# The first block of the merge's second gates is computed as the last filler beside the attention, and the second block stands ahead of the merge, in both layers

## The chip, the cores and the metric

The kernel runs on one core of one Trainium2 chip. The metric is the device time of one execution in microseconds (us). Smaller is better.

## The reference

Two layers of a transformer trunk over 512 latent tokens and 256 context tokens, width 1024, float32. Cut to what matters here, a layer is:

```
h = modulate(rms_norm(x))                              # context tokens: hc, same weights
na_q, na_k, na_v, gq, gk, gv, ga, gb = split(h @ w_in) # ga and gb are 1024 wide each
ya = neighbourhood_attention(na_q, na_k, na_v)         # 8 heads of 64
yb = grouped_query_attention(gq, gk, gv)               # 8 heads of 64
merged = sigmoid(ga) * (ya @ w_pa) + sigmoid(gb) * (yb @ w_pb)
x = x + g1 * (merged @ w_o)
x = x + g2 * swiglu(modulate(rms_norm(x)))
```

The context tokens go through the same steps in layer 0. In layer 1, the last, they only give keys and values. So a product over the tokens covers 768 columns (512 and 256) in layer 0 and 512 in layer 1.

## The kernel before

Activations lie transposed, channels on the partitions and tokens along the free dimension. A float32 product is made of three matmuls for each 128 x 128 weight block: every operand is split into a high half (`hi`, written by ACT) and a low half (`lo`, the rest, written by DVE or POOL), and `steps` (L381) issues high x high, high x low and low x high. A weight is loaded raw (tag `wr`, 4 buffers, 512 KB for a block of 128 output channels), its high half is copied by ACT (`wh`, L366, 3 buffers), and its low half is subtracted by POOL or DVE (`wl`, L368, 3 buffers). In the merge, layer 0 uses POOL and layer 1 uses DVE. Buffers of a tag are handed out in a ring, in the order of the program.

**Attention (`mixing`).** TensorE's order is written out by a planner, `Flow`, while the program is built. The attention of the heads, two per step, is the main line: scores (`sc`), transposes of the softmax (`tp`), products with the values (`y`). Each has to wait for ACT or DVE, and the planner keeps a clock with assumed costs to know when. Beside the main line it keeps a list of fillers, generators that do one projection block each in pieces of three matmuls (`pj`, `pv`): nk, nv and nq are keys, values and queries of the neighbourhood heads, gq queries of the other attention, and gb0 to gb7 the eight blocks of the first branch's gate. A filler's piece goes to TensorE in three cases: when the main line would wait by the planner's clock, when the work done by fillers is behind a pace (`pace`, which spreads the cost of the first and the second group of fillers over the grouped-query and the neighbourhood half of the main line, less a `reserve`), and when a head needs a projection that is not done (`force`). Fillers are taken in the order of `PLAN`'s `fill`. What has been begun and is not finished when the main line ends runs then. A finished gate block is kept in one of the 45 slots of 768 columns that all large tiles share.

**Merge (`merge`).** TensorE's order here comes from the scheduler, which places an instruction when it takes it to be ready. First stands one block of the second gate, ga0 (`GA = 1`, the list `ahead`). The four tiles of yb are read back from DRAM (`yb<-yd`, L1542) and split (L393 on ACT, L394 on DVE). Branch 0 multiplies the eight blocks of w_pb with yb (`pp`) and each result with its gate (`mb`, L1571); all eight gates are ready. Then ya is split (L393, L394), and branch 1 does the same with ga and w_pa. For block 0 the gate is ready, for blocks 1 to 7 a projection of the gate (`pj`) comes before the product. The sum of the branches is split into `mh` and `ml`. Beside this, DVE computes sums for the modulation from transposed weights (`wmodT`, L449), whose raw loads use the same ring `wr`. In layer 0 those are two sums for each weight, in layer 1 one. The row vectors that they multiply (`crow`) are loaded once attention's own pool is free.

The output projection (`po`) and the feed-forward part follow, and then the next layer.

Of the kernel before, what the change touches and what calls it, by code (L numbers as in the profile page):

```python
# [42 lines left out]
for _n in ORDER:  # L43
    for _j in range(COLS[_n][1]):
# [18 lines left out]
BEHIND = 3.0  # L63
SLOTS = 45
ATT_P, ATT_PT = 4, 8
GA = 1

MODS = (((0, 1, 1, 1, 1, 1, 1, 1), (1, 2, 2, 2, 2, 2, 1, 0), (1, 1, 1, 1, 1, 1, 1, 0)),
        ((0, 0, 0, 0, 0, 0, 0, 0), (1, 1, 1, 1, 1, 1, 1, 1), (0, 0, 0, 0, 0, 0, 0, 0)))
# [1 line left out]

PLAN = [
    dict(fill=("nk0 nv0 nq0 gq1 gb0 gq2 gb1 gq3 gb2 gb3 nq1",
               "gb4 nk1 gb5 nq2 nk2 nv1 nq3 nk3 gb6 gb7"),
         early=0.9, reserve=8, hop=0.14, move=3.5, soon=0.5, keep=2,
         busy=12, ctx=0.0, vat=(1, 1), load=2, qt=2, rx=2, slow=(1.1, 1.2, 1), banks="gst", lead=(2, 1, 2), quiet=0.0, spared=0),
    dict(fill=("gq1 gb0 nq0 gq2 nv0 gb1 gq3 gb2 nq1 nk0 gb3",
               "nk1 nk2 nq2 nv1 nk3 gb4 nq3 gb5 gb6 gb7"),
         early=0.8, reserve=2, hop=0.2, move=3, soon=0, keep=2,
         busy=2, ctx=1, vat=(1, 1), load=2.5, qt=2, rx=1, slow=(1, 1, 1), banks="tsg", lead=(2, 2, 1), quiet=28.0, spared=2),  # L80
]
# [13 lines left out]
            g=(0.07, 0.00218, "g"), p=(0.0, 0.19, "g"))  # L95
# [236 lines left out]
class Trunk:  # L332
# [1049 lines left out]
    def mixing(self, l, h, last, at, todo, spare):  # L1382
# [3 lines left out]
        spans = joint[:1] if last else joint  # L1386
        n = spans[-1][1]
        plan = self.plan = PLAN[l]
        block = 3 * D * n // P * COL
        whole = 3 * D * T // P * COL  # L1390
        vals, qs, ya, yb, gates = {}, {}, {}, {}, []
        gqs, keys, bias = at.gqs, at.keys, {}
        self.pbufs = dict(s=1, t=3, g=2)
        yd = [self.dpool.tile([P, T], F32, name=f"yd{l}_{j}") for j in range(4)]
        with ExitStack() as stack:
# [5 lines left out]
            pool = self.att = _Bufs(pool_, dict(rx=plan["rx"], qt=plan["qt"], p=ATT_P, pt=ATT_PT))  # L1401

            self.quiet, self.spared = plan["quiet"], plan["spared"]
            if at.rest:
                todo = self.prologue(l, h, spans, spare, at)
# [5 lines left out]
            def gate():  # L1411
                gates.append(self.slot("gt"))
                return gates[-1]

            gq = [Filler(self.gqa_q(l, j, h, spans, pool, gqs), block, 2) for j in range(1, 4)]
            nk = [Filler(self.na_k(l, j, h, joint, keys), whole, 2) for j in range(4)]
            lead = [Filler(g, 0.0, 0, lead=spare) for g, spare in zip(todo, plan["lead"])]
# [2 lines left out]
            nv = [Filler(self.na_v(l, half, h, vals), 2 * whole, 4) for half in range(2)]  # L1420
            nq = [Filler(self.na_q(l, j, h, spans, qs), block, 4) for j in range(4)]
            gb = [Filler(self.gate(l, "gb", j, h, spans, gate, "g"), block, 1, plan["keep"]) for j in range(KB)]
            named = dict(nk=nk, nv=nv, nq=nq, gb=gb, gq=[None] + gq)
            first, second = [[named[w[:2]][int(w[2])] for w in part.split()] for part in plan["fill"]]

            ctx = 0 if last else 8 * 12 * PASS
# [81 lines left out]
            with tc.manual_schedule(engines={mybir.EngineType.PE}):  # L1508
                flow.run(self.attend(items))
            self.flow = None  # L1510
        return [ya[j] for j in range(4)], yd, gates

    def gate(self, l, what, j, h, spans, make, tag):

# [9 lines left out]

        yield from self.project(w, h, spans, evac, tag)

    def merge(self, l, h, ya, yd, gates, spans, pool, beside):

        nc, d = self.nc, self.d
        n = spans[-1][1]  # L1530
        mb = []
        merged = ([], [])
        yb = []

        ahead = []
        for j in range(GA):
            t = pool.tile([P, T], F32, tag="qt", name=self.name("t"))
            drain(self.gate(l, "ga", j, h, spans, lambda: t, "a"))
            ahead.append(t)
        for t in yd:  # L1540
            yb.append(self.slot("yb"))
            nc.sync.dma_start(yb[-1][:, :n], t[:, :n])  # L1542
        for br, (gname, y) in enumerate((("gb", yb), ("ga", ya))):
            yh = ([], [])
            for t in y:
                hi, lo = self.halves(t[:, :n], n)
                yh[0].append(hi)
                yh[1].append(lo)
            for j in range(KB):
                if br == 0 and j < len(gates):  # L1550
                    t = gates[j]
                elif br == 1 and j < len(ahead):
                    t = ahead[j]
                else:
                    t = pool.tile([P, T], F32, tag="qt", name=self.name("t"))
                    drain(self.gate(l, gname, j, h, spans, lambda: t, "a"))
                w = self.weight(d["wp"][l, 1 - br, j], 512, nc.vector if l else None)
                if beside:
                    for _ in range(MODS[l][br][j]):
                        beside.pop(0)()  # L1560
                if br == 0:
                    mb.append(self.slot("mb"))
                else:
                    hi, lo = self.slot("mh", F32R), self.slot("ml", F32R)
                    merged[0].append(hi)
                    merged[1].append(lo)
                for a, b in spans:
                    pp = self.ps("a", "pp")[:, : b - a]
                    self.gemm(pp, w, yh, a, b, 4)
                    if br == 0:  # L1570
                        nc.vector.scalar_tensor_tensor(mb[j][:, a:b], t[:, a:b], 1.0, pp, op0=ALU.add, op1=ALU.mult)  # L1571
                    else:
                        nc.vector.scalar_tensor_tensor(t[:, a:b], t[:, a:b], 1.0, pp, op0=ALU.add, op1=ALU.mult)
                        nc.vector.tensor_tensor(t[:, a:b], t[:, a:b], mb[j][:, a:b], op=ALU.add)
                        nc.scalar.activation(hi[:, a:b], t[:, a:b], AF.Copy)
                        nc.vector.tensor_tensor(lo[:, a:b], t[:, a:b], hi[:, a:b].bitcast(F32), op=ALU.subtract)
        return merged
# [379 lines left out]
    def run(self):  # L1957
# [3 lines left out]
        with (  # L1961
# [23 lines left out]
            for l in range(DEPTH):  # L1985
# [2 lines left out]
                groups = [(0, 256), (256, 512)] if last else joint  # L1988
                n = spans[-1][1]
                nh = n // 2  # L1990
                ya, yd, gates = self.mixing(l, h, last, at, todo, spare)
                self.pbufs = dict(a=6, n=2)
                with (
                    tc.tile_pool(name=f"psMn{l}", bufs=1, space=PSUM, reuse_waits="tile") as psn,
# [19 lines left out]
                    beside = [one(l, n) for n in range(first, ahead)]  # L2014
                    with tc.tile_pool(name=f"m{l}", bufs=1, reuse_waits="tile") as pool_:
                        pool = _Bufs(pool_, dict(rs=2, qt=5), slots)
                        merged = self.merge(l, h, ya, yd, gates, spans, pool, beside)
                        if not last:
                            self.mod_bias(0, 16, 24)
                            self.gates(0, 0)  # L2020
                        x = []
                        for k in range(KB):
                            x.append(self.slot("x"))
                            nc.sync.dma_start(x[k][:, :n], d["x"][k] if l == 0 else xd[k])
                        right, late = self.out_proj(l, merged, x, nh, pool, beside)
# [79 lines left out]
class Quarters:  # L2105
# [14 lines left out]
    def sum(self, key):  # L2120
        v, at = self.t.nc.vector, self.at
        if key == "S1":
            at["S1"] = self.t.fpool.tile([P, D // 2], F32, tag="ws", name=self.t.name("ws"))[:, : self.n]
            v.tensor_tensor(at["S1"], at["A21"], at["A22"], op=ALU.add)
        elif key == "S2":
            assert "A11" in self.halves
            at["S3"], at["S2"] = at["A21"], at["A11"]
            v.tensor_tensor(at["S3"], at["A11"], at["A21"], op=ALU.subtract)
            v.tensor_tensor(at["S2"], at["S1"], at["A11"], op=ALU.subtract)  # L2129
        elif key == "S4":  # L2130
            assert "A12" in self.halves
            at["S4"] = at["A12"]
            v.tensor_tensor(at["S4"], at["A12"], at["S2"], op=ALU.subtract)
# [170 lines left out]
```

## Time and profile before

| | |
|---|---|
| median of 3 runs | 1966.19 us (1964.42 to 1966.62) |
| profiled execution | 1967.19 us |
| its span, first to last instruction | 1965.1 us |
| mean granted TensorE clock | 0.996 |
| DMA | 214.78 MB, mean 109 GB/s |

PE is TensorE's matmuls, PEld its weight loads, DVE is VectorE, ACT is ScalarE, POOL is GpSimd, and SP is the queue that issues the DMAs. Each profile line of an instruction has its start in us from the span's start, its length, the engine, the line of the kernel, the operation, what it writes and reads, the shape and a count. In brackets stands the idle time before it on its engine, and what ended it. PE's lengths overlap, since matmuls are pipelined. In the trace of before, layer 0's attention ends at about 413 us and its merge at about 551; in layer 1 these are about 1453 and 1542.

### The profile page before, as it was taken

The page shows a single profiled execution, that of the slowest core. Times are in us where ns is not written, and L with a number is a line of the kernel's source. Part 1 is how long each engine was busy: PE and PEld are TensorE (multiplying, and loading weights), DVE is VectorE, ACT ScalarE, POOL GpSimd, SP SyncE. Part 2 cuts the span into 40 slices and gives each one's busy share as a digit, 9 for nine tenths or more (in the row PEclk, how much of TensorE's full clock was granted, in tenths as well). Part 3 has the DMA queues.
Part 4 walks back from the last instruction along what each step waited for, and adds up shares of the span by engine and source line. Part 5 has one row for each costly group of instructions (what it writes and reads, how often), then busy time and mean ns, then how long its engine had stood idle before and what let it go on. Part 6 is the DMA issues. An engine that isn't in the chain of part 4 may idle for free.

```text
span 1965.1 us, 31571 instructions
## 1 busy us (share of the span) xinstructions
PE 1920.8 (98%) x12298; PEld 1777.7 (90%) x12298; DVE 1479.8 (75%) x2813; ACT 948.9 (48%) x1832; POOL 220.1 (11%) x130
## 2 busy tenths in 40 slices
PE   8999999999999999999999999999999999999998
PEld 8989999888899999999999888889888999988997
DVE  7468887788768888786867587879566587876785
ACT  5456666642236534242524255667453364544454
POOL 0332212213200000000000013222300000000000
PEclk9999999999999999999999999999999999999999
DMA  8121112244452143434453422112235532233333
GB/s 324 44 71 41 52 57 63 76 148 166 144 207 86 65 132 127 124 107 138 137 161 116 129 86 60 52 49 78 67 93 196 176 112 77 95 112 96 94 109 108
DMA packets 73109, 214.78 MB, mean 109 GB/s; under 512 B 8704, under 2 KB 10880, under 8 KB 72960
## 3 DMA queue, kind: packets, MB, share of 16 engines
q1 hardware_dynamic: 72960, 212.78, 33.2%
q8 instruction: 96, 1.57, 0.3%
q14 instruction: 53, 0.43, 0.1%
HBM read 200.69 MB, written 6.82 MB: 106 GB/s over the span
## 4 chain that ended last, share of the span: by engine, by line
PE 66%; DVE 6%; issue 3%; ACT 2%; DMA 0%; POOL 0%; DVEq 0%; POOLq 0%; ACTq 0%
PE po L381 19%; PE qu L1726 13%; PE pj L381 10%; PE qv L1726 7%; PE pp L381 4%; PE qc L1726 3%; PE pf L381 3%; PE pv L954 1%; PE sc L1037 1%; PE y L1073 1%; PE tp L1063 1%; PE sc L1164 1%; PE y L1200 1%; DVE w L1593 1%; PE tp L1188 1%
## 5 line engine op out<-in xcount | busy, mean ns | idle before, releaser
L1726 PE MATMUL qu<-r,w 128*128 128x384 f32 (+1 forms) x1872 | 295.4, 310 | 1.9 <-ACT tt L1732 1.9
L1726 PEld LDWEIGHTS qu<-r,w 128*128 128x128 f32 x1872 | 281.1, 189 | 6.5 <-ACT tt L1732 2.7
L381 PE MATMUL pj<-h,wh 128*128 128x512 f32 (+1 forms) x704 | 257.5, 366 | 5.2 <-ACT kg L813 1.7
L366 ACT ACTIVATE wh<-wr 128x1024 fp32r<-128x1024 f32 (+2 forms) x157 | 146.1, 935 | 213.8 <-issue 67.2
L381 PE MATMUL pj<-h,wl 128*128 128x512 f32 (+1 forms) x704 | 247.6, 352 | 0.0
L381 PE MATMUL pj<-hl,wh 128*128 128x512 f32 (+1 forms) x704 | 247.0, 351 | 0.0
L381 PE MATMUL po<-ph,wh 128*128 128x512 f32 (+1 forms) x576 | 197.8, 344 | 2.6 <-ACT wh L366 1.6
L381 PE MATMUL po<-ph,wl 128*128 128x512 f32 (+1 forms) x576 | 196.4, 342 | 2.1 <-DVE wl L368 1.4
L381 PE MATMUL po<-pl,wh 128*128 128x512 f32 (+1 forms) x576 | 195.8, 340 | 0.0
L1589 ACT ACTIVATE w<-wr 128x512 fp32r<-128x512 f32 x234 | 145.4, 625 | 103.5 <-DVE wr L2129 39.3
L368 POOL TENSOR_TENSOR wl<-wr,wh 128x1024 fp32r<-128x1024 f32 (+1 forms) x66 | 144.6, 2194 | 392.8 <-ACT wh L366 392.7
L1581 DVE SCALAR_TENSOR_TENSOR x<-po,G,x 128x256 f32<-128x256 f32 (+3 forms) x168 | 99.1, 596 | 113.4 <-PE po L381 112.4
L1593 DVE TENSOR_TENSOR w<-wr,w 128x512 fp32r<-128x512 f32 x234 | 159.6, 685 | 14.9 <-ACT w L1589 13.6
L1726 PE MATMUL qv<-r,w 128*128 128x384 f32 (+1 forms) x936 | 151.1, 310 | 1.7 <-ACT tt L1732 1.7
L381 PEld LDWEIGHTS pj<-h,wh 128*128 128x128 f32 x704 | 134.0, 190 | 20.2 <-ACT kg L813 1.9
L381 PEld LDWEIGHTS pj<-h,wl 128*128 128x128 f32 x704 | 133.4, 189 | 18.2
L381 PEld LDWEIGHTS pj<-hl,wh 128*128 128x128 f32 x704 | 134.2, 191 | 13.8
L1726 PEld LDWEIGHTS qv<-r,w 128*128 128x128 f32 x936 | 141.1, 190 | 2.8 <-ACT tt L1732 2.7
L1013 ACT ACTIVATE pth<-tp 128x512 fp32r<-128x512 f32 x176 | 103.4, 595 | 65.3 <-PE tp L1063 37.7
L509 POOL TENSOR_TENSOR rs<-rs,expo 128x2 f32<-128x2 f32 (+2 forms) x8 | 6.2, 773 | 1116.7 <-DVE rs L508 1116.7
L1014 DVE TENSOR_TENSOR ptl<-tp,pth 128x512 fp32r<-128x512 f32 x176 | 119.5, 685 | 15.1 <-ACT pth L1013 13.4
L381 PEld LDWEIGHTS po<-ph,wh 128*128 128x128 f32 x576 | 108.4, 188 | 17.5 <-ACT wh L366 3.5
(249 smaller groups left out, 4321.2 us busy)
## 6 DMA issues: line engine op xcount, KB each, us to landing
wr<-wfi SPq DMA_DIRECT2D x88, 512.0 KB, 3.3
wr<-wmodT SPq DMA_DIRECT2D x84, 512.0 KB, 3.3
wr<-win SPq DMA_DIRECT2D x68, 512.0 KB, 3.3
wr<-wfo SPq DMA_DIRECT2D x64, 256.0 KB, 2.7
wr<-wo SPq DMA_DIRECT2D x26, 512.0 KB, 3.6
wr<-wfo SPq DMA_DIRECT2D x26, 384.0 KB, 3.3
wr<-wp SPq DMA_DIRECT2D x32, 256.0 KB, 2.9
x<-x SPq DMA_DIRECT2D x16, 384.0 KB, 6.4
```

The lines of the kernel that those rows point to most:

```text
L366: nc.scalar.activation(hi, raw, AF.Copy)
L368: (eng or nc.gpsimd).tensor_tensor(lo, raw, hi[:].bitcast(F32), op=ALU.subtract)
L381: nc.tensor.matmul(ps[:, : b - a], u[:, c], v[k][:, a:b], start=(k == 0 and i == 0), stop=(k == nk - 1 and i == 2),)
L954: nc.tensor.matmul(ps[:, t * 256 : t * 256 + 256], a[k][:, tok], b[:, c], start=(k == 0 and i == 0), stop=(k == KB - 1 and i == 2))
L1013: nc.scalar.activation(hi, tp, AF.Copy)
L1014: nc.vector.tensor_tensor(lo, tp, hi[:].bitcast(F32), op=ALU.subtract)
L1037: nc.tensor.matmul(s[:, lo:up], qt[:, b * P : (b + 1) * P], kk[k][:, lo:up], start=(k == 0 and (b % 2 == 0 or lo > 0)), stop=(k == 1), ski ...
L1063: nc.tensor.transpose(tp[:, (2 * j + b) * P : (2 * j + b + 1) * P], ps_[b][:, (k + j) * P : (k + j + 1) * P], self.ident)
L1581: self.nc.vector.scalar_tensor_tensor(x[j][:, f:u], ps[:, f - a : u - a], self.G[l][i][:, s, j : j + 1], x[j][:, f:u], op0=ALU.mult, op1=A ...
L1589: self.nc.scalar.activation(t[:, :n], src, AF.Copy)
L1593: self.nc.vector.tensor_tensor(t[:, n : 2 * n], src, t[:, :n].bitcast(F32), op=ALU.subtract)
L1726: nc.tensor.matmul(banks[bank], u[:, c], v, start=(first and k == 0 and i == 0), stop=(k == kn - 1 and i == 2), skip_group_check=True)
```

## The change

One block of ga moves into the list of fillers of both layers, as the last one. It is kept in a slot (list `others`) and handed to `merge` as the first entry of `ahead`. The block that `merge` computes before its loops is now ga1. Branch 1 finds the gates of blocks 0 and 1 ready and computes six. `GA[l]` is the pair of the blocks beside attention and the blocks ahead of the merge.

```diff
-GA = 1
+
+GA = (1, 1), (1, 1)
...
     dict(fill=("nk0 nv0 nq0 gq1 gb0 gq2 gb1 gq3 gb2 gb3 nq1",
-               "gb4 nk1 gb5 nq2 nk2 nv1 nq3 nk3 gb6 gb7"),
+               "gb4 nk1 gb5 nq2 nk2 nv1 nq3 nk3 gb6 gb7 ga0"),
...
     dict(fill=("gq1 gb0 nq0 gq2 nv0 gb1 gq3 gb2 nq1 nk0 gb3",
-               "nk1 nk2 nq2 nv1 nk3 gb4 nq3 gb5 gb6 gb7"),
+               "nk1 nk2 nq2 nv1 nk3 gb4 nq3 gb5 gb6 gb7 ga0"),
...
+            def other():
+                others.append(self.slot("gt"))
+                return others[-1]
...
+            ga = [Filler(self.gate(l, "ga", j, h, spans, other, "g"), block, 1, plan["keep"]) for j in range(GA[l][0])]
+            named = dict(nk=nk, nv=nv, nq=nq, gb=gb, ga=ga, gq=[None] + gq)
...
-    def merge(self, l, h, ya, yd, gates, spans, pool, beside):
+    def merge(self, l, h, ya, yd, gates, ahead, spans, pool, beside):
...
-        ahead = []
-        for j in range(GA):
+        for j in range(GA[l][0], sum(GA[l])):
             t = pool.tile([P, T], F32, tag="qt", name=self.name("t"))
             drain(self.gate(l, "ga", j, h, spans, lambda: t, "a"))
             ahead.append(t)
...
-                        merged = self.merge(l, h, ya, yd, gates, spans, pool, beside)
+                        merged = self.merge(l, h, ya, yd, gates, others, spans, pool, beside)
```

More of the change, by code (lines that the diff above doesn't have):

```diff
@@ L1390, in mixing @@
         whole = 3 * D * T // P * COL
-        vals, qs, ya, yb, gates = {}, {}, {}, {}, []
+        vals, qs, ya, yb, gates, others = {}, {}, {}, {}, [], []
         gqs, keys, bias = at.gqs, at.keys, {}
@@ L1422, in mixing @@
             gb = [Filler(self.gate(l, "gb", j, h, spans, gate, "g"), block, 1, plan["keep"]) for j in range(KB)]
-            named = dict(nk=nk, nv=nv, nq=nq, gb=gb, gq=[None] + gq)
+            ga = [Filler(self.gate(l, "ga", j, h, spans, other, "g"), block, 1, plan["keep"]) for j in range(GA[l][0])]
+            named = dict(nk=nk, nv=nv, nq=nq, gb=gb, ga=ga, gq=[None] + gq)
             first, second = [[named[w[:2]][int(w[2])] for w in part.split()] for part in plan["fill"]]
@@ L1510, in mixing @@
             self.flow = None
-        return [ya[j] for j in range(4)], yd, gates
+        return [ya[j] for j in range(4)], yd, gates, others
     def gate(self, l, what, j, h, spans, make, tag):
@@ L1990, in run @@
                 nh = n // 2
-                ya, yd, gates = self.mixing(l, h, last, at, todo, spare)
+                ya, yd, gates, others = self.mixing(l, h, last, at, todo, spare)
                 self.pbufs = dict(a=6, n=2)
```

## The prediction

> **What bounds the kernel now.** First the page's busy shares, then one table of stretches around the two places where attention ends and the branch merge begins, then the chain of waits, then TensorE's own timeline there. In the table the columns behind the stretch are its length, the busy time of PE, weight loads, DVE, ACT and POOL, the granted PE clock, the DMA share and GB/s.
>
> ```profile
> PE 1920.8 (98%) x12298; PEld 1777.7 (90%) x12298; DVE 1479.8 (75%) x2813; ACT 948.9 (48%) x1832; POOL 220.1 (11%) x130
> ```
> ```profile
> 407.40:413.30 5.90, 4.21 (x28) 3.42 (x27) 5.79 (x10) 4.85 (x10) 1.92 (x1) 0.96 0.23 77
> 413.30:416.60 3.30, 3.30 (x11) 2.63 (x10) 1.01 (x3) 1.28 (x2) 0.00 (x0) 0.56 0.81 259
> 423.00:456.60 33.60, 33.60 (x195) 29.66 (x194) 31.01 (x49) 7.23 (x11) 13.03 (x8) 1.00 0.55 188
> 456.60:464.05 7.45, 6.14 (x27) 4.49 (x25) 7.32 (x13) 2.64 (x4) 1.29 (x1) 1.00 0.38 122
> 1459.20:1481.10 21.90, 21.89 (x97) 17.80 (x95) 13.62 (x20) 7.18 (x11) 0.00 (x0) 1.00 0.42 129
> 1481.10:1482.50 1.40, 0.40 (x2) 0.35 (x3) 1.40 (x4) 1.40 (x4) 0.00 (x0) 1.00 0.86 312
> ```
>
> TensorE is busy 98% of the span, and the change neither adds nor removes a matmul. So only TensorE's idle and slow time can be won or lost, 44.3 us of the span in all, and of that only what lies near the moved work. In layer 0 the tail of attention (407.40 to 413.30) has 1.69 us idle, and the 3.30 us behind it run at a clock of 0.56. The first branch (423.00 to 456.60) is full, and between the branches 1.31 us are idle (456.60 to 464.05) with DVE busy 7.32 of 7.45. Layer 1 has only the small hole of 1.00 us at 1481.
>
> **The change part by part.** *The price of a block.* The chain of waits gives start, length, work:
>
> ```profile
> 471.36 4.18 PE pp L381 x24
> 475.54 8.34 PE pj L381 x48
> ...
> 1453.15 6.18 PE pj L381 x27
> ...
> 1493.28 5.44 PE pj L381 x24
> 1498.71 2.72 PE pp L381 x12
> ```
>
> A gate block (pj) is 8.34 us of TensorE in layer 0 and 5.44 in layer 1; a branch product (pp) is 4.18 and 2.72. Before, ga0 stands between attention and the first branch and ga1 to ga7 in the second branch. After, ga0 is the last filler of attention, ga1 stands between, and six blocks remain behind. Each block brings its 512 KB load, an ACT copy for the high half (below the one of ga1, at 452.42), a low half and a tanh for each span:
>
> ```profile
> 452.42 1.06 ACT L366 ACTIVATE wh<-wr 128x1024 fp32r<-128x1024 f32 x1 [3.55 <-PE pp L381]
> 456.60 0.63 ACT L366 ACTIVATE wh<-wr 128x512 fp32r<-128x512 f32 x1 [1.65 <-POOL wl L368]
> ```
> ```profile
> L1522 ACT ACTIVATE t<-pj x24: 361/578/599, 420.4 to 1540.3; 128x512 f32<-128x512 f32 x16, 128x256 f32<-128x256 f32 x8
> ```
> ```profile
> L368 POOL TENSOR_TENSOR wl<-wr,wh 128x1024 fp32r<-128x1024 f32 (+1 forms) x66 | 144.6, 2194 | 392.8 <-ACT wh L366 392.7
> ...
> wr<-win SPq DMA_DIRECT2D x68, 512.0 KB, 3.3
> ```
>
> Inside attention the low half goes to POOL in both layers (late in layer 1 too), about 2.2 us on an engine that works 11% of the span; in layer 1 that takes one such operation from DVE. I cost these at nothing: they run ahead under the last blocks of gb. Without that cover ga0 would start up to 3.3 + 1.06 + 2.2 = 6.6 us late. The extra slot that ga0 holds (one of 45) is also costed at nothing: the reload of yb could be held back by it, but ga1's 8.34 us still stand ahead of the first branch.
>
> *Where ga0 goes, layer 0.* The fillers run out before attention does:
>
> ```profile
> 407.29 0.28 PE L381 MATMUL pj<-h,wl 128*128 128x256 f32 x1
> 407.42 0.60 PE L1112 MATMUL tp<-ident_sb,p 128*128 128x128 f32 x4
> 407.83 0.77 PE L1200 MATMUL y<-pth,v 128*128 128x256 f32 x5
> ...
> 410.22 0.51 PE L1122 MATMUL y<-pth,v 128*128 128x256 f32 x2 [0.24 <-DVE ptl L1014]
> 410.56 0.40 PE L1122 MATMUL y<-ptl,v 128*128 128x256 f32 x2
> 412.13 0.47 PE L1122 MATMUL y<-pth,v 128*128 128x256 f32 x2 [1.17 <-DVE y L1024]
> 412.76 0.79 PE L1122 MATMUL y<-ptl,v 128*128 128x256 f32 x2 [0.16 <-DVE ptl L1014]
> 413.35 0.63 PE L381 MATMUL pj<-h,wh 128*128 128x512 f32 x1
> ```
>
> The last piece of gb7 is at 407.29. After it stand the last transposes and value products with three waits, and ga0 only from 413.35. The two heads that need nq3 and nk3 force all fillers before gb6 to be done, in both versions, so that point is the same and what follows it is filled by waits: gb6 and gb7 are used up at 407.29 as before, and ga0 then goes into the waits. A piece of it is three matmuls. The idle here is 1.69 us; in layer 1, where fillers do not run out, the same kinds of pieces take 1.10 (ten y) and 0.46 (four tp):
>
> ```profile
> 1448.40 1.10 PE y L1200 x10
> 1449.51 0.46 PE tp L1188 x4
> ```
>
> So the 5.93 us from 407.42 to 413.35 would need 2 x 0.46 + 1.10 + about 0.9 for the eight y of L1122 (estimate, 8/10 of 1.10) = 2.9; the loss is between the 1.69 shown idle and 3.0. I take 2.2 gained, since the longest wait (1.17) comes from DVE being late with the halves of yb, which the filling plan does not count, and may not be asked to cover.
>
> *The slow stretch.* The first matmul of ga0 is 0.63 long; at 0.56 of the clock 3.30 us hold 3.30 x 0.44 = 1.45 us too much. It follows a stretch with 71% busy (4.21 of 5.90). If that is filled the clock should stay: 1.4 gained, bounds 0 and 1.45. The Trainium skill, TensorE: Matmul & The Clock Gate, "HAM oscillation — how this bites in real kernels", puts the limit at idle gaps above about 3.4 us. No single gap here is above 1.17 us and the clock fell all the same, so the trace does not agree; by that rule the slow stretch would not hang on these gaps and would stay, and the sum below would be -0.8 instead of -2.2. I go by the row.
>
> *Between the branches, layer 0.* What is late next is the split of ya on DVE, which the second branch needs:
>
> ```profile
> 457.72 0.50 PE L381 MATMUL pj<-h,wh 128*128 128x512 f32 x1 [0.73 <-DVE mb L1571]
> 464.05 0.50 PE L381 MATMUL pp<-lo,wh 128*128 128x512 f32 x1 [0.58 <-DVE lo L394]
> ```
> ```profile
> 454.96 2.10 DVE L449 CUSTOM_DVE_ANT_0 junk<-wr,crow 128x1024 f32<-128x1024 f32 x1 [2.13 <-DMA wr<-wmodT]
> 463.05 0.95 DVE L394 TENSOR_TENSOR lo<-y,hi 128x768 fp32r<-128x768 f32 x1
> ```
> ```profile
> 447.31 0.33 SPq L357 DMA_DIRECT2D wr<-win  x1
> 447.74 0.37 SPq L357 DMA_DIRECT2D wr<-wp  x1
> 451.61 0.81 SPq L357 DMA_DIRECT2D wr<-wmodT  x2
> ```
>
> Before, TensorE ran out of branch-0 products at 456.60, did the first span of ga1 (from 457.72), and met the first low half of ya at 464.05. After, ga1 has been done earlier and cannot stand here. But the first branch ends later: 456.60, plus 8.34 for ga1, minus 3.6 (2.2 + 1.4) from the tail = 461.3. DVE's queue of modulation sums starts from attention's last transposes, not from ga0's end, so it does not move with them, and its 2.13 us wait for a load goes, because ga1's raw weight (447.31) leaves the four-buffer load ring in front of those two loads: low half at 464.05 - 2.1 = 461.9. On the other side, the ring is emptied by TensorE's progress through branch 0, and could hold the sums back by up to the 8.34 - 3.6 = 4.7 us that TensorE is later, giving 468.8 less 2.1 = 466.7. Idle between the branches is then 0.6 to 5.4 us against 1.31. I take 1.5, near the early end, since DVE is the fuller engine there (31.01 of 33.60) and the extra time goes to it first: +0.2. The time of ga1's first span is not lost: it was spent before.
>
> *Between the branches, layer 1.*
>
> ```profile
> 1482.10 0.50 PE L381 MATMUL pp<-hi,wh 128*128 128x512 f32 x1 [1.01 <-ACT hi L393]
> 1482.44 0.40 PE L381 MATMUL pj<-h,wh 128*128 128x512 f32 x1
> ```
> ```profile
> 1481.44 2.18 ACT L393 ACTIVATE hi<-y 128x512 fp32r<-128x512 f32 x4
> ```
> ```profile
> 1482.96 2.49 DVE L394 TENSOR_TENSOR lo<-y,hi 128x512 fp32r<-128x512 f32 x4
> ```
>
> TensorE waits 1.01 us for the upper half of ya, does one matmul, then ga1 while DVE makes the lower halves. After, no gate is ready in that place: ga2's weights need the ring buffer that the last product of branch 0 frees. The second matmul waits for the first lower half, 1482.96 + 2.49/4 = 1483.6, that is 2.5 us after 1481.10 less the one matmul of 0.3: 2.2 idle instead of 1.0, +1.2. Bounds: -1.0 (halves come in time because the scheduler places them earlier) and +2.7 (1.2 and a clock drop of 1.45 as at 413.30). Layer 1's tail of attention gains nothing: the chain has 27 pj without a hole there, three of gb7 and ga0.
>
> *The rest of attention.* The second group of fillers is longer by one block and is handed out faster. That could fill, or make, waits like these, 1.0 each; I take 0, bounds -2.0 and +2.0:
>
> ```profile
> PE tp L1188 <- DVE z L1007: 1.0, 1, 1.0
> ```
> ```profile
> PE pv L954 <- DVE ql L988: 1.0, 1, 1.0
> ```
>
> *The sum*: -2.2 - 1.4 + 0.2 + 1.2 + 0 = -2.2 us. The profiled run took 1967.19 us (span 1965.1 and 2.1 around it), 1.0 above the median of the runs, 1966.19. Set against the median: 1964.0. Less than 0.2% (3.9 us) is about what a measurement of this kernel cannot tell from no change.
>
> **The rivals.** *Everything closes (0.25).* The halves of ya come in time in both layers and the tail closes fully: -3.0 - 1.45 - 1.31 - 1.01 = -6.8, with attention's own waits down to -8.8: 1957.4 to 1962, middle 1960. For it: DVE has a third of its time free in layer 1's first branch (13.62 of 21.90), and the halves of ya are ready to be made long before. Against it: they were ready early in this version too, and were placed at the branch's end.
>
> *The cover is lost (0.14), on the slower side.* One place: the start of layer 0's second branch. If the splits of ya keep their distance from branch 0's end, TensorE stands 7.45 us where ga1 stood, 6.1 more than now, and the clock drops behind it (+1.4). With layer 1's +1.2 and the tail's -3.6 that is +5.1: 1971.3. It decides once the lower half comes 3.7 us behind the last product of branch 0 (3.6 - 1.2 + 1.3, where the sum is zero); from 6.2 on, with the clock drop, the loss passes 0.2%. For it: the next gate, ga2, can't fill in early, since its copy comes only at the ring's turn at branch 0's end, as at 456.60, and another 2.2 us on POOL follow. Against it: 2.13 us of DVE's delay is a load that comes sooner now.
>
> *Nothing moves (0.13).* The plan sees no wait in layer 0's tail, runs ga0 behind the last value product as the merge did, and the gap between the branches absorbs the rest: -1 to +1.5, 1966.
>
> **How the numbers follow.** The forecast has 0.48, its own range 1962 to 1966.5. Faster by over 0.2% (under 1962.3) is the first rival and 0.06 of the forecast: 0.31. Slower by over 0.2% (over 1970.1) is most of the second: 0.12. Within: 0.57. The range for 8 in 10 runs from 1959.0, inside the first rival, to 1970.0, which leaves most of the second out.
>
> **What would show it.** Right: in layer 0 pieces of pj stand between the last tp and y, no stretch at 0.56 follows, two gates' worth of pj precede the first pp, and TensorE idles 1 to 3 us where the second branch begins, waiting for lo. In layer 1 the wait of pp for hi turns into one for lo, 2 us or so. Wrong: a wait of over 5 us for lo in layer 0, a clock drop behind either gap, ga0 waiting for its weights, yb reloaded so late that the first pp waits, or new waits inside attention's second half.

## The result, and the profile after

The changed kernel takes 1969.84 us (median of 18 runs, 1965.38 to 1974.34), the kernel before 1965.11 us (18 runs, 1961.82 to 1966.62). The ratio is 1.0025, 95% interval 1.0019 to 1.0031: slower by 4.7 us, where 2.2 us faster was forecast. The profiled execution of after took 1967.43 us (span 1965.7), only 0.24 us more than that of before; why the two profiles hide the difference is told below.

Stretches of the two kernels from landmark to landmark (those called before and after are the kernel before and the changed one): end of layer 0's scores to the first branch product, from there to the first product of out_proj, then for layer 1 the last value product to the first branch product, and from there to out_proj. The columns are those of the prediction's table. Before:

```profile
401.70:423.00 21.30, 19.61 (x122) 17.38 (x121) 16.57 (x29) 12.56 (x27) 1.92 (x1) 0.92 0.35 120
423.00:550.50 127.50, 126.19 (x723) 110.67 (x722) 103.85 (x159) 33.48 (x56) 37.92 (x21) 1.00 0.46 157
1452.90:1459.20 6.30, 6.30 (x31) 5.24 (x30) 3.67 (x7) 3.75 (x8) 0.00 (x0) 1.00 0.36 125
1459.20:1542.10 82.90, 81.89 (x362) 67.48 (x361) 51.87 (x74) 29.67 (x44) 0.00 (x0) 1.00 0.48 159
```

After:

```profile
402.20:428.20 26.00, 26.00 (x173) 23.73 (x172) 14.55 (x29) 14.47 (x30) 2.58 (x2) 1.00 0.39 134
428.20:551.00 122.80, 119.12 (x674) 104.47 (x674) 107.71 (x160) 31.96 (x53) 37.10 (x20) 0.99 0.47 159
1449.00:1459.30 10.30, 10.30 (x48) 8.58 (x47) 3.82 (x7) 4.14 (x7) 0.00 (x0) 1.00 0.65 205
1459.30:1542.40 83.10, 78.71 (x337) 64.34 (x337) 50.47 (x73) 28.09 (x41) 0.00 (x0) 0.96 0.47 152
```

A gate block is 8.34 us in layer 0 and 5.44 in layer 1. Six blocks instead of seven remain in each merge, so the two should have come out at 127.5 - 8.34 = 119.2 and 82.9 - 5.44 = 77.5 us. They took 122.8 and 83.1: 3.6 and 5.6 us were lost in them. The loss lies where the branches meet. There, in after:

```profile
407.40:418.30 10.90, 10.90 (x73) 9.85 (x72) 4.25 (x11) 4.95 (x11) 1.29 (x1) 1.00 0.59 208
461.85:480.00 18.15, 14.47 (x66) 11.65 (x65) 17.43 (x30) 3.16 (x4) 3.29 (x2) 0.91 0.48 166
1481.30:1500.00 18.70, 14.35 (x53) 11.39 (x54) 9.71 (x15) 6.47 (x10) 0.00 (x0) 0.82 0.42 139
```

The tail of layer 0's attention (407.40 to 418.30) is now full at full clock, as forecast. But 3.68 of the 18.15 us behind branch 0 of layer 0 are idle, and 4.35 of the 18.70 us behind that of layer 1, and the clock falls to 0.91 and 0.82 there.

**Layer 0's boundary.** TensorE, ACT and DVE in after:

```profile
466.50 0.50 PE L382 MATMUL pj<-h,wh 128*128 128x512 f32 x1 [2.86 <-ACT wh L367]
458.18 1.56 ACT L394 ACTIVATE hi<-y 128x768 fp32r<-128x768 f32 x2
465.39 1.06 ACT L367 ACTIVATE wh<-wr 128x1024 fp32r<-128x1024 f32 x1 [5.65 <-DMA wr<-win]
466.09 0.95 DVE L395 TENSOR_TENSOR lo<-y,hi 128x768 fp32r<-128x768 f32 x1
```

TensorE ends branch 0 at about 462. The first low half of ya has its turn in DVE's queue only at 466.09 and is done at 467.04, 5 us later, although ACT made the high halves from 458.18 on. In the kernel before the low half came even later after branch 0's end (456.60 to 464.00), but ga1's product stood in between. Matmuls of ga2 are written ahead of the product that needs the low half, so TensorE also waits for ga2's weight. In this profile that wait of 2.86 us ended at 466.50 with ACT's copy, for whose load ACT had waited 5.65 us, and the low half came 0.5 us behind it: both were late. The load was itself issued only at 460.93, after the load queue had waited 2.9 us for DVE, whose sum begun at 458.70 ended just before.

**Layer 1's boundary.** TensorE, ACT, DVE and the load queue in after:

```profile
1483.11 0.73 PE L382 MATMUL pp<-hi,wh 128*128 128x512 f32 x2 [1.85 <-ACT hi L394]
1486.85 0.79 PE L382 MATMUL pj<-h,wl 128*128 128x512 f32 x1 [2.54 <-DVE wl L369]
1481.48 1.06 ACT L367 ACTIVATE wh<-wr 128x1024 fp32r<-128x1024 f32 x1 [2.49 <-DMA wr<-win]
1482.44 2.17 ACT L394 ACTIVATE hi<-y 128x512 fp32r<-128x512 f32 x4
1484.42 1.22 DVE L450 CUSTOM_DVE_ANT_0 wr<-wr,crow 128x1024 f32<-128x1024 f32 x1 [2.43 <-DMA wr<-wmodT]
1485.58 1.22 DVE L369 TENSOR_TENSOR wl<-wr,wh 128x1024 fp32r<-128x1024 f32 x1
1486.71 2.49 DVE L395 TENSOR_TENSOR lo<-y,hi 128x512 fp32r<-128x512 f32 x4
1477.27 0.33 SPq L358 DMA_DIRECT2D wr<-win  x1
1479.93 0.33 SPq L358 DMA_DIRECT2D wr<-wmodT  x1
```

Here the queues are in the way. ga2's raw weight is issued at 1477.27. ACT waits 2.49 us for it, with ya's high halves queued behind its copy: TensorE idles 1.85 us. DVE waits 2.43 us for a load of the sums that was issued at 1479.93, behind ga2's weight, and has ga2's low half and then ya's low halves queued behind that: TensorE idles 2.54 us more.

**Why the profiles look equal.** TensorE's clock drops in one execution and not in another, for a few us at a time, behind waits that both have: in layer 1's attention TensorE waits 1.66 us until about 1204 and 1.91 us until about 1295, in both profiles (until 1204.38 and 1295.70 in before, 1203.78 and 1293.50 in after). The stretches around these waits in the profile of before:

```profile
1200.00:1205.00 5.00, 3.34 (x26) 3.09 (x25) 2.62 (x9) 3.73 (x7) 1.64 (x1) 0.97 0.00 0
1205.00:1210.00 5.00, 5.00 (x30) 4.60 (x30) 3.59 (x9) 3.38 (x7) 0.00 (x0) 0.69 0.02 5
1290.00:1295.00 5.00, 3.78 (x31) 3.39 (x29) 4.78 (x9) 2.22 (x5) 0.00 (x0) 1.00 0.24 54
1295.00:1300.00 5.00, 4.30 (x21) 4.01 (x22) 3.61 (x9) 2.50 (x5) 0.00 (x0) 0.69 0.00 0
```

and, behind the same two waits, in that of after:

```profile
1205.00:1210.00 5.00, 5.00 (x43) 4.86 (x43) 4.69 (x10) 4.57 (x10) 0.00 (x0) 1.00 0.01 3
1295.00:1300.00 5.00, 5.00 (x38) 4.69 (x38) 4.42 (x10) 2.82 (x5) 0.77 (x1) 1.00 0.00 0
```

Layer 1's scores and values took 258.6 us in the profile of before. In three other executions with the same layer 1 they took 255.4, 257.0 and 258.3; with the changed layer 1, in the 15 profiled executions, between 255.3 and 258.8. One profile of each kernel can't show a difference of 4 us in the whole; its stages can.

### The profile page after: what moved, and what is told of

The parts are those of the page before. It is cut to its first block, busy times and chain, and to the rows that moved or that the text cites. A ratio compares the mean times of both kernels' runs of the same rounds, so it can differ in the third digit from the quotient of the medians.

```text
span 1965.7 us, 31561 instructions
## 1 busy us (share of the span) xinstructions
PE 1919.4 (98%) x12298; PEld 1777.2 (90%) x12298; DVE 1480.5 (75%) x2812; ACT 950.3 (48%) x1832; POOL 223.8 (11%) x131
## 4 chain that ended last, share of the span: by engine, by line
PE 66%; DVE 6%; issue 2%; ACT 1%; DMA 1%; POOL 0%; DVEq 0%; POOLq 0%; ACTq 0%
PE po L382 20%; PE qu L1731 13%; PE pj L382 11%; PE qv L1731 7%; PE pp L382 3%; PE qc L1731 3%; PE pf L382 3%; PE pv L955 1%; PE y L1074 1%; PE sc L1038 1%; PE tp L1064 1%; PE y L1201 1%; PE sc L1165 1%; PE tp L1189 1%; DVE w L1598 1%
```

## The experiments

All times are medians beside runs of the kernel before on the same chip; a ratio is to those, with its 95% interval. "Boundary" is the place between the branches, "stage" the time from a layer's first branch product to out_proj's first. The runs are called e1 to e18. What each was expected to show stands ahead of its result.

**1. One layer at a time (e1, e2).** Which layer loses? In e1 layer 1 is unchanged, `GA = (1, 1), (0, 1)` and no ga0 in the second layer's list:

> The change in layer 0 alone; layer 1 is as before (ga0 ahead of the merge, seven blocks behind). Theory M: the loss sits where the second branch begins, because no finished gate block is left to run there while ya is split, and TensorE stands in its written order in front of ga2, whose weights come late through the load ring. Layer 0 then shows what the profile of the changed kernel shows: about 3.1 us won in attention's tail and 3.7 us lost between the branches, together +0.6 us, between -1 and +2.5 us against before. Rival R: the loss is clock drops and waits in attention, from the longer list of fillers and the extra slot; then layer 0's merge is not what costs, and this kernel is 2 to 3 us slower with the lost time ahead of 410 us.

Measured: 1967.54 us, ratio 1.0016 (1.0008 to 1.0025). In e2 layer 0 is unchanged instead, `GA = (0, 1), (1, 1)` and no ga0 in the first layer's list:

> The change in layer 1 alone; layer 0 is as before. Theory M: layer 1's tail of attention has nothing to win, and between the branches TensorE stands over 4 us with half the clock behind it: 5.6 us lost in the merge, 0 to 1 us won in attention, so +4.0 to +5.6 us, most of the 4.7 us that the whole change costs. Rival R: under 2.5 us, spread over attention.

Measured: 1968.60 us, ratio 1.0018 (1.0009 to 1.0027). Both layers lose, about 2.4 and 3.4 us; the first is at the upper end of what was expected, the second somewhat under it. TensorE's longest wait in the stage (total, times, longest), first layer 0 of the one, then layer 1 of the other:

```profile
PE pj L382 <- DVE mb L1576: 4.8, 1, 4.8
```
```profile
PE pj L382 <- DVE wl L369: 2.7, 1, 2.7
```

The first run has the same layer 0 as after and idled 5.5 us at its boundary where after's profile idled 3.7. Its stage took 125.3 us. Section 7 comes back to the difference.

**2. No block between attention and merge (e3).** Is the block that remains there needed? `GA = (1, 0), (1, 0)`:

> Only half of the change: ga0 is the last filler of attention in both layers, and no block stands ahead of the merge; ga1 is computed in the second branch, as in the kernel before. Theory M: ga1 is back as the block that runs while ya is split, so the gaps between the branches shrink to about those of before in layer 1 (1 us); what is left of ga0 behind attention's end covers the split of yb in both layers. Layer 0's tail keeps its 3.1 us: 1 to 4 us faster than before. Rival C: the block ahead of the merge is needed as cover for the reload and split of yb, and its absence costs 2 to 5 us of idle time in front of the first product of the first branch, with a clock drop behind: 0 to 5 us slower than before.

Measured: 1967.99 us, ratio 1.0015 (1.0006 to 1.0023). ga1 covers the boundary again, but now branch 0 itself waits, for its own halves and weights (layer 0):

```profile
PE pp L382 <- DVE lo L395: 3.1, 2, 2.0
PE pp L382 <- POOL wl L369: 1.3, 1, 1.3
```

Without a block there DVE, POOL and ACT are late at the start; with it they are late at the boundary.

**3. Sums later (e4, e5).** Are the modulation sums in the way? Those of the second branch moved to its later blocks. Each entry of the kernel's list `MODS` says for how many transposed weights the sums are done beside one block. Such a weight is called a sum below; in layer 0 it is two passes of DVE. Cut from that list:

```diff
-(1, 2, 2, 2, 2, 2, 1, 0)   # layer 0, branch 1
+(0, 0, 2, 2, 2, 2, 2, 2)
-(1, 1, 1, 1, 1, 1, 1, 1)   # layer 1, branch 1
+(0, 0, 1, 1, 1, 1, 2, 2)
```

> The changed kernel with the modulation sums of blocks 0 and 1 of the second branch moved to its later blocks (layer 0: 0,0,2,2,2,2,2,2 instead of 1,2,2,2,2,2,1,0; layer 1: 0,0,1,1,1,1,2,2 instead of one each). Their loads no longer stand ahead of ga2's raw weights in the four-buffer ring, nor the sums ahead of ya's low halves on DVE. Theory M, with the ring as the reason: ga2's weights and ya's halves come 3 to 4 us earlier in layer 0 and 2 to 3 us earlier in layer 1, the gaps fall under 1.5 us each, and the kernel is 3 to 5 us faster than the changed one, 0 to 2 us faster than before or equal to it. If the load ring is not the reason and it is only that ga1 is missing there, the gaps stay at 3 to 5 us and the time is that of the changed kernel.

Measured: 1971.22 us, ratio 1.0033 (1.0020 to 1.0045). Layer 1's stage fell from 83.1 to 77.9. Layer 0's boundary stayed open (5.8 us of waiting for lo), and out_proj waited at the end of layer 0's second branch. So the edit was repeated in layer 1 alone, as e5:

> The changed kernel with the column sums beside layer 1's merge moved to its later blocks (0,0,1,1,1,1,2,2 instead of one a block), layer 0 as changed. Theory A, the loss of layer 1 lies in the order of loads and splits at its branch boundary: first product of branch 1 of layer 1 to the first product of out_proj 77.9 us (83.1 in the changed kernel, 77.9 in the earlier run with both layers' sums moved), idle at the boundary under 2 us, no other stage of layer 1 longer; the whole about 5 us under the changed kernel: 1965.0, that is 0.0 +- 1.5 against the kernel before. Rival R, the two kernels' difference is the clock falling by chance and not the boundaries: the stage gets shorter but the median stays at 1968 or more.

Measured: 1965.41 us, ratio 0.9998 (0.9989 to 1.0007) where after has 1.0025, that is 4 to 5 us under after. Layer 1's boundary has one wait left:

```profile
1484.70:1503.00 18.30, 16.98 (x75) 14.07 (x76) 14.20 (x21) 7.63 (x12) 0.00 (x0) 1.00 0.56 186
```
```profile
PE pp L382 <- ACT hi L394: 1.4, 1, 1.4
```

1.32 us idle instead of 4.35, and the clock stays at 1.00. That settles layer 1: the loads and sums queued ahead of ya's halves held TensorE up. All later runs have this edit, except the next one (e6) and the two controls on the kernel before (e11 and e16).

**4. Layer 0: is it the late yb (e6, e7, e8)?** In after, yb's halves are made after ga0's first tanh and not, as before, between the last probabilities; DVE's first sum is 10 us later. The first high half of yb in before, and all four in after:

```profile
404.62 0.86 ACT L393 ACTIVATE hi<-yb 128x768 fp32r<-128x768 f32 x1
```
```profile
417.44 0.60 ACT L1528 ACTIVATE gt<-pj 128x512 f32<-128x512 f32 x1
417.94 0.84 ACT L394 ACTIVATE hi<-yb 128x768 fp32r<-128x768 f32 x1
420.84 2.30 ACT L394 ACTIVATE hi<-yb 128x768 fp32r<-128x768 f32 x3
```

The 45 slots are handed out in program order, and the slot of ga0 (first written at 417.44) stands ahead of those of yb and its halves. The edit hands these out first, in layer 0:

```diff
             def other():
+                if l in (0,):
+                    for t in yd:
+                        early.append(self.slot("yb"))
+                        nc.sync.dma_start(early[-1][:, :n], t[:, :n])
+                    early[:] = [self.halves(t[:, :n], n) for t in early]
                 others.append(self.slot("gt"))
...
```

`merge` then takes these halves instead of making its own.

> The changed kernel; in layer 0 alone the slots of yb, its reload and its halves are traced ahead of the slot of the second gates' first block, so that ACT and DVE have the yb halves again between the last probabilities of the attention. Theory A, DVE's queue comes 10 us late in the changed kernel because the slot for the extra gate is handed out first: yb halves from about 406 us (417.9 in the changed kernel), first column sum at about 426 (431.8), first product of branch 0 to out_proj's first product 119.5 to 121 us (122.8 and 125.3 in two runs of the changed layer 0), idle at layer 0's branch boundary under 2 us; the whole 3 to 5 us under the changed kernel, about 1966. Rival B, it is the third block's raw weight that comes late through the ring, or PE's written order, not DVE: the halves move, but the stage stays at 123 to 126 us with 4 us or more idle at 462 to 480, and the whole at 1969 to 1970.

Measured: 1969.77 us, ratio 1.0024 (1.0014 to 1.0033). The halves moved as meant (first at 405.22), the first sum came at 426.4 (431.8 in after), and nothing was won:

```profile
PE pp L382 <- DVE lo L395: 3.8, 1, 3.8
```
```profile
464.12 2.49 DVE L395 TENSOR_TENSOR lo<-y,hi 128x768 fp32r<-128x768 f32 x1
462.41 3.38 POOL L369 TENSOR_TENSOR wl<-wr,wh 128x1024 fp32r<-128x1024 f32 x1 [3.12 <-ACT wh L367]
```

My theory A fell here, as the reason for the whole wait. Nor was it the load of ga2's weight, whose copy ended at 462.34 in this run while TensorE stood until 466.66. But the low half itself took 2.49 us where it takes 0.95 elsewhere, beside POOL's work on ga2's weight: some 1.5 of the 3.8 us come from there (section 7). With layer 1's edit as well (e7), and then with the reload one gate earlier (e8):

> Both of the edits before this together: layer 0's yb halves ahead of the gate's slot, layer 1's sums in later blocks. Theory A: both losses are gone and what the change was to gain shows: layer 0 -3 us and layer 1 -1 us against the kernel before, 1961.5 (1960 to 1963). Rival B: as the run with layer 1's sums alone, 1965.

Measured: 1964.61 us, ratio 0.9998 (0.9989 to 1.0007).

> As the run with both mended, with layer 0's yb reload issued one gate earlier (at the last first gate), some 6 us sooner, so that ACT cannot stand waiting for it in the attention's tail. If the reload's landing (about 406 us) holds ACT up there, this one is 1 to 2 us shorter than the run before it; if not, the two agree within 0.5 us.

Measured: 1965.08 us, ratio 0.9998 (0.9990 to 1.0007). Both as the run with layer 1's edit alone (e5).

**5. Layer 0: is it the amount of DVE's work (e9 to e12)?** In e9 two sums are taken out of branch 0 (they are done beside the FFN):

```diff
-(0, 1, 1, 1, 1, 1, 1, 1)   # layer 0, branch 0
+(0, 1, 1, 1, 1, 1, 0, 0)
```

> The changed kernel with layer 1's sums later, and the last two column sums beside layer 0's first branch taken out of the merge (0,1,1,1,1,1,0,0; they are done beside the FFN instead, no work is left out). Theory C, in layer 0 the vector engine is full all through the first branch, and its sums, not the halves of yb, set when the low half of ya comes; what stood between the branches before, the second block's 8.34 us, hid that. Two sums are 4 passes of 1.2 to 2.1 us, so the low half comes 5 us or more sooner, at 461 to 462: idle at 462 to 480 under 1.5 us, first product of the first branch to out_proj's first 119.3 to 120.5 us (125.0 with the sums in), the whole 1961 +- 1.5. Rival B, the third block's late weight and the written order hold TensorE there: the stage stays at 123 us or more and the whole at 1965.

Measured: 1964.91 us, ratio 0.9999 (0.9990 to 1.0007). The stage fell to 118.1, the boundary is closed, and the FFN gave it all back. The stage and layer 0's FFN here, then the FFN of before:

```profile
428.70:546.80 118.10, 117.48 (x674) 103.30 (x673) 99.17 (x152) 31.79 (x53) 38.36 (x20) 1.00 0.46 156
651.30:1090.70 439.40, 434.24 (x2474) 415.15 (x2473) 343.25 (x590) 163.71 (x291) 0.00 (x0) 0.99 0.38 126
```
```profile
655.00:1088.70 433.70, 433.17 (x2479) 414.14 (x2477) 338.06 (x582) 163.54 (x291) 0.00 (x0) 1.00 0.39 125
```

439.4 against 433.7 us; 5.2 us of it is one wait of TensorE there for the low half of a weight on DVE. The next three runs are e10, the same with yb's halves early; e11, the control on the kernel before; and e12, which is e10 with a third sum moved:

> As the run with fewer sums in layer 0, with layer 0's yb halves ahead of the gate's slot as well. Theory C: the boundary is closed already by the fewer sums, so this one agrees with it within 0.7 us (stage 119 to 120). If the place of yb's halves matters beside the sums, it is 1 to 2 us shorter.

Measured: 1978.76 us, ratio 1.0066 (1.0050 to 1.0082). The boundary was open again (3.5 us for lo): with the loads in another order DVE stood 5.8 us waiting for the raw loads of the sums in branch 0. Another 8 us went at layer 1's start (113.2 us from the FFN's end to the first scores, 105.2 in the other runs), where TensorE waited 6.0 us for a residual of DVE.

> The kernel before with the same two sums taken out of layer 0's first branch: a control. Theory C: there the second block's product covers the vector engine's queue, 1.3 us are idle at the boundary, so it gains at most 1.3 us: 1964 to 1966. If fewer sums are simply good for any kernel (the merge bound by the vector engine all through), it gains 3 us or more: 1962 or less.

Measured: 1970.13 us, ratio 1.0023 (1.0014 to 1.0032). Layer 0's stage is 127.4, as in before (127.5): there is nothing to win there when ga1 stands at the boundary. The FFN took 439.4 here too, which the expectation had left out.

> As the run with fewer sums and yb's halves first, with one more sum moved from the end of layer 0's first branch to the end of its second (0,1,1,1,1,0,0,0 and 1,2,2,2,2,2,1,1). Theory C: once the boundary is closed a third sum less is worth nothing there (stage 119 to 120, the whole within 0.7 us of that run), or 1 us is lost where the second branch ends.

Measured: 1972.75 us, ratio 1.0034 (1.0022 to 1.0046), stage 125.1, 5.4 us waiting for lo. Fewer sums, and not closed: with yb's halves early DVE again waited 3.4 us for such a load, and the pass that came then took 2.64 us. The amount alone does not decide either.

**6. All sums kept in the merge (e13 to e16).** The two sums moved to blocks 2 and 3 of layer 0's second branch (e13), to its last two blocks (e14), and one sum alone (e15):

```diff
-(0, 1, 1, 1, 1, 1, 1, 1), (1, 2, 2, 2, 2, 2, 1, 0)
+(0, 1, 1, 1, 1, 1, 0, 0), (1, 2, 3, 3, 2, 2, 1, 0)   # first
+(0, 1, 1, 1, 1, 1, 0, 0), (1, 2, 2, 2, 2, 2, 2, 1)   # second
+(0, 1, 1, 1, 1, 1, 1, 0), (1, 2, 2, 2, 2, 2, 2, 0)   # third
```

> The changed kernel with layer 1's sums later, and layer 0's last two sums of the first branch moved to blocks 2 and 3 of the second: (0,1,1,1,1,1,0,0), (1,2,3,3,2,2,1,0). Theory C, the vector engine's work in branch 0 holds the low half of ya: layer 0's stage from the first product of the first branch to out_proj's first is 118 to 120 us (118.1 in the run with fewer sums, 125.0 with the sums in), the FFN's stage stays 432.9, and the whole is 1958 to 1960, the first version faster than both kernels. Rival D, it is the order of loads and sums: blocks 2 and 3, with three sums and a gate's weight in a ring of four, now wait for their loads, the stage is 121 or more and the whole 1962 or more.

Measured for e13: 1961.48 us, ratio 0.9977 (0.9967 to 0.9987): the version that beats both kernels. The stage, what follows it to the FFN, and TensorE's wait at the boundary:

```profile
427.20:545.60 118.40, 117.49 (x675) 103.31 (x674) 105.09 (x157) 31.68 (x53) 38.67 (x20) 1.00 0.48 160
545.60:653.60 108.00, 104.87 (x602) 102.22 (x601) 85.42 (x163) 54.18 (x98) 1.70 (x2) 1.00 0.38 132
```
```profile
PE pp L382 <- DVE lo L395: 0.9, 1, 0.9
```

118.4 us as expected; but out_proj (108.0, 104.5 before) gives 3.5 us back, waiting for DVE, so the whole is 1.5 us over the expected 1960.

> The same with the two sums in the last two blocks of layer 0's second branch instead: (1,2,2,2,2,2,2,1). Theory C: the boundary is closed as well (under 1 us idle), and the end of the branch decides: 118 to 120 us if out_proj's first weights are not held up, some 2 to 5 us lost there otherwise, as in the run with both layers' sums moved; the whole 1959 to 1963.

Measured: 1968.03 us, ratio 1.0013 (1.0004 to 1.0023), stage 123.5, boundary 3.7 us idle, and 110.2 us from there to the FFN (104.5 in before).

> The same with one sum moved, (0,1,1,1,1,1,1,0) and (1,2,2,2,2,2,2,0). Theory C, in proportion to the work: one sum is 2.4 to 4.2 us of the vector engine, so the low half comes 2.5 to 4 us sooner and about half of the 5 us idle is left, stage 120.5 to 122.5, the whole 1961 to 1963. Rival D: no proportion.

Measured: 1966.53 us, ratio 1.0001 (0.9992 to 1.0009), stage 124.8, boundary 5.4 us idle. There is no proportion to the work moved.

The last one, e16, is a control on the kernel before:

> A control, the kernel before with the sums of layer 0 as in e13: (0,1,1,1,1,1,0,0), (1,2,3,3,2,2,1,0). Theory C: the second block covers the vector engine's queue at the boundary there, 1.3 us idle are all there is to win: 1964 to 1966. If the sums alone make the difference it is as fast as e13.

Measured: 1966.02 us, ratio 0.9994 (0.9984 to 1.0003). The kernel before gains nothing from layer 0's sums as the fastest version has them; it takes the change and the sums together. Layer 1's later sums, which e13 also has, were not tried on the kernel before, whose boundary there has 1.0 us idle.

**7. What separates the open boundary from the closed one (e17, e18).** The runs of 6 with two sums moved, e13 (closed) and e14 (open), have the same written order on DVE up to ya's low halves. In e14, DVE and POOL:

```profile
458.63 2.27 DVE L450 CUSTOM_DVE_ANT_0 junk<-wr,crow 128x1024 f32<-128x1024 f32 x1 [0.29 <-DMA wr<-wmodT]
463.11 0.17 DVE L476 TENSOR_SCALAR G<-mod 128x8 f32<-128x8 f32 x1
463.18 0.68 DVE L1576 SCALAR_TENSOR_TENSOR mb<-gt,pp 128x512 f32<-128x512 f32 x1
463.78 1.74 DVE L476 TENSOR_SCALAR G<-mod 128x8 f32<-128x8 f32 x1
465.44 0.95 DVE L395 TENSOR_TENSOR lo<-y,hi 128x768 fp32r<-128x768 f32 x1
458.54 1.29 POOL L369 TENSOR_TENSOR wl<-wr,wh 128x512 fp32r<-128x512 f32 x1 [2.88 <-ACT wh L367]
463.14 2.35 POOL L369 TENSOR_TENSOR wl<-wr,wh 128x1024 fp32r<-128x1024 f32 x1 [3.32 <-ACT wh L367]
```

The operation of 128x8 elements that takes 0.17 us at 463.11 takes 1.74 at 463.78, and ends when POOL's low half of ga2's weight does (463.14 + 2.35 = 465.49). ya's low half stands behind it. The sum at 458.63, begun just after POOL's operation at 458.54, takes 2.27 us instead of 1.22. In e13 the first low half was just ahead of POOL (461.40, POOL from 461.90). The product with a gate, which reads one operand from PSUM, is not stretched (0.68 at 463.18). The Trainium skill, SBUF — State Buffer, "Who interferes with whom", says that a VectorE instruction with two SBUF inputs, or in a two-port mode, and a GpSimd instruction that reads SBUF block each other for the whole instruction, by who starts first; these rows agree with it.

Other open runs show the same. In e1 an operation of 128x8 elements took 2.31 us at 465.82 (POOL worked from 465.71), in e15 one took 2.31 us at 465.33 (POOL from 464.56), in e10 one took 2.35 us; in e5 ya's first low half itself took 2.61 us. In e1, which has the layer 0 of after, that makes about 2 of the 5.5 us idle: `mb`, for which TensorE waited 4.8 us, stood right behind it. In after's own profile POOL began on ga2's weight at 466.53, behind the start of the low half, so this did not come in: the 3.7 us idle there are the lag of DVE's queue, with one pass of 2.20 us in it, and of ga2's weight.

To test it, ga2's low half went from POOL to DVE in layer 0, behind ya's first two low halves, in e14 (as e17) and in e13 (as e18):

> e14 with one operation on another engine: the low half of the third block's weight (128x1024) in layer 0 is made by the vector engine, behind the first two low halves of ya, instead of by GpSimd beside them. Theory E, vector operations that start while GpSimd works are held until it ends: the 128x8 operation of 1.74 us takes about 0.17, the first low half of ya is done at about 464.8 us after the same start (466.4 in e14), idle at the boundary 2.1 us (3.7 in e14), the whole 1.5 to 3 us less than e14: 1965 to 1966.5. Rival C alone, only the amount of work counts: the vector engine has 1.2 us more to do and the boundary stays at 3.7 us or grows.

```profile
460.78 0.17 DVE L476 TENSOR_SCALAR G<-mod 128x8 f32<-128x8 f32 x1
460.86 0.95 DVE L395 TENSOR_TENSOR lo<-y,hi 128x768 fp32r<-128x768 f32 x1
```
```profile
PE pp L382 <- DVE lo L395: 0.6, 1, 0.6
PE pj L382 <- DVE x L1586: 6.4, 1, 6.4
```

The operation took 0.17 us, the boundary fell to 0.6 us idle and the stage to 117.9 (123.5). The boundary won 3.1 us, more than the 1.6 expected: the sum that takes 2.27 us in e14 was not stretched in this run either, though the edit leaves POOL's operation beside it in place. By these rows 1.6 us are the edit's, and the rest is a shift of the two queues. Against the expected 1965 to 1966.5, the whole took 1973.57 us, ratio 1.0037 (1.0025 to 1.0050): at layer 1's start TensorE waited 6.4 us for a residual of DVE (113.4 us where e14 takes 105.3). The written order there is the same, but the first matmul of the projection carries a wait on DVE that it does not carry in e14. Why was not followed up.

> The same edit on e13. Theory E: the second low half of ya, 2.83 us in e13, takes 0.95; but TensorE waits for the first one alone there (0.9 us idle), which was ahead of GpSimd already, so the boundary stays at 0.5 to 1 us and the whole within 1 us of e13, 1960.5 to 1962.5. If the vector engine's extra 1.2 us counts, the end of the branch is 1 us longer.

Measured: 1961.64 us, ratio 0.9981 (0.9972 to 0.9990), stage 117.8, boundary 0.6: as expected, within 0.2 us of e13. The stage is 0.6 us shorter and out_proj 1.7 longer (109.7): TensorE waits there 3.1 us for low halves of weights on DVE, 1.5 in e13.

## Why the prediction was wrong, step by step

The time, 1969.84, lies just inside the end of the wide range (1970.0). That is luck as far as the sum goes: the path was that of the rival *The cover is lost*, not that of the forecast.

- *ga0 into layer 0's tail* (-2.2) was right: no idle is left there, and last score to first product grew by 4.7 us (21.3 to 26.0), that is 8.34 - 3.6 with the next step.
- *The slow stretch* (-1.4) was a chance of the profiled run. Three other executions with the same layer 0 tail (e2, e11, e16) took 19.7, 19.7 and 21.3 us for what took 21.3 in before: two of them have no slow stretch. On average half of the term was there to win. I weighed the Trainium skill's limit of 3.4 us (TensorE: Matmul & The Clock Gate, "HAM oscillation — how this bites in real kernels") against a single run: a drop without any gap of that length does happen, but not each time.
- *Between the branches, layer 0* (+0.2) is the step that failed. It said that DVE's queue starts from attention's last transposes and does not move with TensorE, and so put the low half at 461.9; the late bound was 466.7, and 467.04 was measured. The queue did move: the first half of yb, the silu of crow and the first sum came 13, 7 and 10 us later in after. Even with yb's halves put back (e6) the sums started 4.6 us later than in before (426.4 against 421.9), about as much as TensorE: there ACT made the silu of crow at 420.30, right behind ga0's second tanh at 420.04, where in before it came at 415.70, when crow's load ended. By that order the sums hang on TensorE's ga0, which the step had ruled out. What ga1's 8.34 us covered there before was 7.4 us of DVE's lag; the rival *The cover is lost* had the mechanism. Its price for layer 0 was a little high: against the 119.2 us due, three runs with this layer 0 (122.8, 125.3, 125.0) lost 3.6 to 6.1 us, where the rival had 6.1 + 1.4. The prediction did not have POOL's hold on DVE at all, which makes some of the difference between these runs. Also, the row at 456.60 that it gave for the turn of ga2's copy is that of a 128x512 weight of a branch product; ga2's copy came at 465.39.
- *The extra slot*, costed at nothing, did hold yb's reload and halves back by 13 us, behind ga0's own slot. That it costs no time is right as far as e6 shows: putting it right gained nothing, though POOL's hold on the low half cost some 1.5 us in that run.
- *Between the branches, layer 1* (+1.2, upper bound +2.7) was mis-sized. The stage lost 5.6 us. The step counted the first low half at DVE's speed and no queue in front of it; a load of ga2 on ACT and a load of the sums on DVE, 2.49 and 2.43 us of waiting, stood ahead of ya's halves. Without the sums there (e5) the boundary has 1.3 to 1.4 us idle, where the step had 2.2, and the stage is 77.9, 0.4 over the 77.5 due.
- *The rest of attention* (0, +-2) held: layer 0's scores took 307.9 us instead of 308.6, and layer 1's attention scatters alike in both kernels. Layer 1's attention and ga0 together grew by about 1.5 us less than a block, which was costed at nothing.

The sum, from the stages with their scatter averaged: layer 0 won 0.7 in the scores and 2.0 to 3.6 in the tail and lost 3.6 to 6.1 in the merge; layer 1 won 1.5 in attention and lost 5.6. The middles sum to -0.7 - 2.8 + 4.9 - 1.5 + 5.6 = +5.5 us, against 4.7 measured. What stays open is which operations of DVE meet POOL's in a given version. The outcome at layer 0's boundary (0.6 to 5.8 us) flips with shifts of about 1 us between e13 and e14, and I could not forecast it from the trace of before.

## What to carry to other kernels

A block of work that stands at a boundary hides the lag of every other queue there; before moving it, add up what DVE, ACT and the load queue still owe at that point, with all that is queued ahead of the operand that is needed next. When work moves ahead, move the side work (here the modulation sums) out of the boundary that it uncovered as well: the change alone cost 4.7 us, layer 0's sums alone gained nothing, and the change with both layers' sums moved gained 4.5 us. Read the loss from stages of several runs, not from the whole of two profiles.

## What the hardware showed that I had not expected

- A tiny vector operation (128x8) can take 1.74 us instead of 0.17 when it starts while GpSimd works, and ends when that does (e14); moved off GpSimd, the same work left it at 0.17 (e17).
- The granted clock dropped to 0.69 for 5 us behind waits of 1.66 and 1.91 us in one execution and stayed at 1.00 behind the same waits in another. Each drop costs some 1.5 us (estimate, 5.00 x 0.31). The 18 executions of before scatter by 4.8 us and those of after by 9.0, and of the latter the shortest has a mean clock of 0.997, the longest one of 0.992.
- Two sums moved beside the FFN cost some 6 us there (439.4 against about 433 in the changed kernel), more than the 4.9 us (estimate, 4 x 1.22) that their four passes take on DVE alone.
